# A two-layer encoder trunk: the order of the opening, four float32 products, and one more seven-product chunk

## The chip, the cores and the metric

The kernel runs on one core of one Trainium2 chip. The metric is device microseconds of one execution, lower is better; the time of a kernel is the median of its runs. The engines are TensorE (PE: products; PEld: its weight loads), VectorE (DVE), ScalarE (ACT), GpSimd (POOL) and SyncE (SP), whose queue issues nearly all the transfers.

## The reference, cut to what matters

```python
SEQ, D_MODEL, D_FF, DEPTH = 256, 1024, 2816, 2
def swiglu(h, w_gate, w_up, w_down):
    return (jax.nn.silu(h @ w_gate) * (h @ w_up)) @ w_down

for i in range(DEPTH):
    h = rmsnorm(x, ffn1_norm[i])
    x = x + 0.5 * swiglu(h, ffn1_w_gate[i], ffn1_w_up[i], ffn1_w_down[i])
    h = rmsnorm(x, mix_norm[i])
    proj = h @ w_in[i]                    # q, k, v of self attention, q of memory attention
    ...                                   # self attention (another kind in each layer), memory attention
    x = x + jnp.concatenate([o_s, o_m], axis=-1) @ w_out[i]
    h = rmsnorm(x, ffn2_norm[i])
    x = x + 0.5 * swiglu(h, ffn2_w_gate[i], ffn2_w_up[i], ffn2_w_down[i])
```

All data are float32. The four feed-forward blocks hold most of the work: 256 rows of x by three matrices of 1024 x 2816 each.

## The kernel before, in words

**Three passes for one product.** TensorE multiplies in the type fp32r. A matrix is split into `hi`, its cast to fp32r (ScalarE), and `lo`, the rest (VectorE: raw minus `hi`), and a product is the sum of three passes, hi by hi, lo by hi and hi by lo, each 128 x 128 by 128 x 512 (`dense`, L511, L514, L517). The weights come in chunks of 1 MB into one of three `raw` buffers and are split there in four units (`split_hi`, L338, and `split_lo`, L356), into one of four pairs of buffers (`hl_left`); x is transposed on TensorE (`prep_half`: four transposes L525 into `xtp`, scaled to `y` on VectorE at L557, split into `xh`, at L560, and `xl`, at L562), for each half `tb` of the 256 rows and each half `hf` of the 1024 columns.

**A feed-forward block** (`ffn`) goes through 11 groups of 256 hidden columns, gate and up side by side in 512. K = 1024 is cut into two chunks `c` of four K tiles `k`, so a group is two weight chunks, each 4 tiles x 2 halves of rows x 3 passes = 24 products, which collect in the two banks `gu`. `evac` makes the hidden values and turns them round through DRAM (`hb`, `hd`, `hr`). Two neighbouring groups (`pair`) are done by a scheme of seven products of sums in place of eight; its sums of x (`pair_forms`) overwrite `y`. Then comes the down projection, 11 chunks of 24 products into four banks `acc`.

**Seven-product chunks.** Down chunks listed in `SEVEN` do with 7 x 3 products what otherwise takes 8 x 3: VectorE forms four sums of weights (`wsum`, L350), and seven units are split in place of four; of the hidden values it forms four sums (`sf`, L681) and seven split forms (`h`, L690 and L694) in place of one `ht` (L665, L667). The first such chunk of a block has two `hi` and two `lo` buffers; the later ones are guests (`guest`): their last three units go to `gxh` and `gxl`, the room of the transposed x, free in a down projection. There is one such room (`xt_room`), given back by the seventh product of a guest.

**The order.** The schedule is manual. A planner in Python (`Flow`) walks through the products in the order written in `ffn` and `mixer`, keeps a clock with guessed durations, and emits the other engines' instructions as its threads' conditions and times come due; each engine then runs its own list in that order and waits on semaphores for data and buffers. The loader's guess of arrivals is `dma_free` and `LAT`. At the start TensorE runs `warm` products of the identity, which are not used.

Of the kernel before, what the change touches and what calls it, by code (L numbers as in the profile page):

```python
# [20 lines left out]
P = 128  # L21
# [19 lines left out]
T_MM = 0.216  # L41
# [101 lines left out]
def kernel(  # L143
# [41 lines left out]
    def load_x(tb, hf, queue=None):  # L185
        (queue or nc.sync).dma_start(out=xs[tb][:, hf * 512:(hf + 1) * 512],
                                     in_=x[0, tb * P:(tb + 1) * P, hf * 512:(hf + 1) * 512])

    load_x(0, 0)
    load_x(1, 0, nc.scalar)  # L190
# [18 lines left out]
    def loaded():  # L209
        n = len(late_loads)  # L210
        yield lambda: late_done[0] >= n
        yield flow.now + 8.0
# [34 lines left out]
    class Item:  # L247
# [27 lines left out]
    dma_free = [2.5]  # L275
# [10 lines left out]
    def loader():  # L286
        for i, c in enumerate(chunks):
# [4 lines left out]
            n = len(c.parts)  # L292
            for j, (dst, src) in enumerate(c.parts):
                nc.sync.dma_start(out=dst(c.raw), in_=src)
                dma_free[0] += 2.9 / n
                if i < 2 and j % 2:
                    for q in range((j - 1) * 4 // n, (j + 1) * 4 // n):
                        c.block[q] = dma_free[0] + LAT
                if i == 1 and j == 1:
                    load_x(1, 1)  # L300
                    dma_free[0] += 0.7
            c.arrive = dma_free[0] + LAT
# [39 lines left out]
    def split_lo():  # L342
        for i, it in enumerate(items):
# [8 lines left out]
            for src, q, w, dep in it.units:  # L352
                yield lambda: it.hit[q] is not None
                yield it.hit[q]
                yield calm_v(i)
                nc.vector.tensor_sub(it.part(1, q, w), src(), it.part(0, q, w).bitcast(F32))  # L356
                t = flow.dve(512 * w)
                it.lot[q:q + w] = [t] * w
            raw_left[0] += it.frees
# [17 lines left out]
    SEVEN = {(0, 1): (), (0, 2): (1, 4, 7), (1, 1): (1, 4, 7), (1, 2): (1, 4, 7)}  # L377
# [64 lines left out]
    def plan_ffn(l, nm, wg, wu, wd):  # L442
# [8 lines left out]
        work = [(g, c) for g in range(NG) for c in range(2)]  # L451
        if pair is not None:
# [70 lines left out]

    def turn(dst, src, flipped=False):
        nc.tensor.transpose(out=dst, in_=src, identity=flip if flipped else ident)  # L525
        return flow.pe(T_TR)
# [9 lines left out]
    class Xt:  # L536
        def __init__(self, keep=False):
# [7 lines left out]
            self.keep, self.y, self.ft = keep, {}, [None] * 4  # L545

    def prep_half(xt, tb, hf, gc, wait=0.0):
# [11 lines left out]
        yield flow.dve(512)  # L559
# [3 lines left out]
        if xt.keep:  # L563
            xt.y[tb, hf] = y
        else:
            g2.give()
# [51 lines left out]
    def ffn(l, nm, xt, gc_next):  # L618
# [151 lines left out]
        def pair_forms():  # L770

            yield lambda: len(xt.y) == 4 and g4.left >= 4
# [76 lines left out]
        if (l, nm) != (0, 1):  # L849
            for tb in range(2):  # L850
                for c in range(2):
                    plain_chunk(0, c, (tb,))
        else:
# [775 lines left out]
    def start_gain():  # L1629
# [5 lines left out]
        flow.dve(16)  # L1635
        warm(2)
        yield 4.6
        warm(5)
# [12 lines left out]
    table_hint(AF.Silu)  # L1651
# [67 lines left out]
```

## Time and profile before

| | |
|---|---|
| runs before | 955.98 us median of 3 (955.21 to 956.04) |
| the profiled execution | 955.69 us; its span, first to last instruction, 953.9 us |
| TensorE | busy 945.6 us (99% of the span), 4475 records |
| VectorE, ScalarE, GpSimd | busy 820.0 (86%), 587.0 (62%), 109.1 us (11%) |
| transfers | 204.04 MB, mean 214 GB/s |

Times in the profile count from the first instruction. A row of the timeline has start, duration, engine, line of the kernel, operation, output<-inputs, shape and count; in brackets stand the idle time of the engine before it and what ended that. A float32 product that is no transpose shows as two records. A product's record lasts longer than its place in the row of products, since neighbours overlap: the cost of one is the spacing of the starts.

### The profile page before, as it was taken

To read this page: it belongs to the slowest core of one execution; us is meant where nothing else is said; L and a number is where in the kernel's file an instruction comes from. 1 tells how busy PE (TensorE), PEld (TensorE's weight loads), DVE (VectorE), ACT (ScalarE), POOL (GpSimd) and SP (SyncE) were. 2 spreads that over 40 slices of the span, in tenths; PEclk is the share of its full clock that TensorE was granted. 3 is DMA by queue.
4 is the path that set the end of the run, shared out by engine and by line. 5 is a ranking of instruction groups with operands and counts; after the bars stand their busy time and mean duration, and the time that the engine had idled before them with its cause. 6 is when DMAs were issued, how large, how long until landed. Compare 5 with 4: busy or idle time off the path is not lost.

```text
span 953.9 us, 13334 instructions
## 1 busy us (share of the span) xinstructions
PE 945.6 (99%) x4475; PEld 774.1 (81%) x4475; DVE 820.0 (86%) x1483; ACT 587.0 (62%) x1121; POOL 109.1 (11%) x160
## 2 busy tenths in 40 slices
PE   9999999999999999999999999999999999999998
PEld 7888888887777888888888888888787778888886
DVE  7898978888777899979889899796999888999884
ACT  6556566677676746647546656564676865665650
POOL 1000057621210100000000000000434200000000
PEclk9999999999999999999999999999999999999999
DMA  8987799486525387887746679775641367588751
GB/s 265 289 263 236 224 354 296 158 276 210 177 90 177 97 266 225 262 287 219 245 146 219 208 226 288 247 253 166 196 158 57 121 214 228 183 275 276 239 197 45
DMA packets 169887, 204.04 MB, mean 214 GB/s; under 512 B 10137, under 2 KB 145114, under 8 KB 169818
## 3 DMA queue, kind: packets, MB, share of 16 engines
q1 hardware_dynamic: 169498, 202.78, 66.0%
q8 instruction: 35, 0.57, 0.3%
q10 hardware_dynamic: 320, 0.40, 0.1%
q14 instruction: 34, 0.28, 0.1%
HBM read 188.99 MB, written 14.16 MB: 213 GB/s over the span
## 4 chain that ended last, share of the span: by engine, by line
PE 90%; DVE 6%; DMA 2%; ACT 1%; issue 1%; SPq 0%; ACTq 0%; DVEq 0%
PE gu L517 13%; PE gu L514 13%; PE gu L511 13%; PE acc L511 9%; PE acc L517 9%; PE acc L514 9%; PE pair_m L511 3%; PE pair_m L514 3%; PE pair_m L517 3%; PE pj L517 2%; PE pj L511 2%; PE pj L514 2%; DVE lo L356 2%; PE S L1360 1%; DMA x<-in_x_dram 1%; PE AV L1441 1%
## 5 line engine op out<-in xcount | busy, mean ns | idle before, releaser
L338 ACT CAST hi<-raw 128x512 fp32r<-128x512 f32 (+1 forms) x467 | 336.3, 770 | 172.6 <-DMA raw<-in_ffn_w_up_dram 45.6
L356 DVE TENSOR_TENSOR lo<-raw,hi 128x512 fp32r<-128x512 f32 (+1 forms) x467 | 391.9, 875 | 35.5 <-ACT hi L338 35.4
L514 PE MATMUL gu<-lo,xh 128*128 128x512 f32 x576 | 224.7, 390 | 0.5 <-DVE lo L356 0.5
L517 PE MATMUL gu<-hi,xl 128*128 128x512 f32 x576 | 224.5, 390 | 0.4 <-DVE xl L562 0.4
L511 PE MATMUL gu<-hi,xh 128*128 128x512 f32 x576 | 224.4, 390 | 0.0
L517 PEld LDWEIGHTS gu<-hi,xl 128*128 128x128 f32 x576 | 108.1, 188 | 23.9 <-DVE xl L562 1.7
L514 PEld LDWEIGHTS gu<-lo,xh 128*128 128x128 f32 x576 | 108.1, 188 | 23.5 <-DVE lo L356 1.4
L511 PEld LDWEIGHTS gu<-hi,xh 128*128 128x128 f32 x576 | 108.2, 188 | 22.3
L517 PE MATMUL acc<-hi,ht 128*128 128x512 f32 x280 | 109.5, 391 | 0.0
L511 PE MATMUL acc<-hi,ht 128*128 128x512 f32 x280 | 109.2, 390 | 0.0
L514 PE MATMUL acc<-lo,ht 128*128 128x512 f32 x280 | 109.1, 390 | 0.0
L338 ACT CAST hi<-wsum 128x512 fp32r<-128x512 f32 x82 | 47.7, 619 | 26.5 <-DVE wsum L350 26.5
L514 PE MATMUL pj<-lo,xh 128*128 128x512 f32 x160 | 64.0, 400 | 0.0
L517 PE MATMUL pj<-hi,xl 128*128 128x512 f32 x160 | 63.8, 399 | 0.0
L511 PE MATMUL pj<-hi,xh 128*128 128x512 f32 x160 | 63.8, 399 | 0.0
L514 PEld LDWEIGHTS acc<-lo,ht 128*128 128x128 f32 x280 | 52.6, 188 | 10.9
L517 PEld LDWEIGHTS acc<-hi,ht 128*128 128x128 f32 x280 | 52.6, 188 | 10.8
L511 PEld LDWEIGHTS acc<-hi,ht 128*128 128x128 f32 x280 | 52.6, 188 | 10.7
L532 POOL TENSOR_TENSOR xr<-v,nhalf 128x1 f32<-128x1 f32 x12 | 10.3, 861 | 435.1 <-DVE v L530 435.1
L356 DVE TENSOR_TENSOR lo<-wsum,hi 128x512 fp32r<-128x512 f32 x82 | 52.8, 680 | 0.0
L633 ACT ACTIVATE sil<-gu,xr 128x256 f32<-128x256 f32 x72 | 33.7, 468 | 29.8 <-PE gu L517 29.7
L532 POOL TENSOR_TENSOR hf<-v,nhalf 128x8 f32<-128x8 f32 (+1 forms) x20 | 31.4, 1570 | 87.3 <-DVE v L530 78.9
(232 smaller groups left out, 1429.5 us busy)
## 6 DMA issues: line engine op xcount, KB each, us to landing
raw<-in_ffn_w_down_dram SPq DMA_DIRECT2D x176, 256.0 KB, 4.5
raw<-in_ffn_w_gate_dram SPq DMA_DIRECT2D x82, 512.0 KB, 4.0
raw<-in_ffn_w_up_dram SPq DMA_DIRECT2D x82, 512.0 KB, 5.4
raw<-in_w_in_dram SPq DMA_DIRECT2D x32, 512.0 KB, 4.4
hd<-hb SPq DMA_DIRECT2D x44, 256.0 KB, 4.6
hr<-hd SPq DMA_DIRECT2D x44, 256.0 KB, 4.6
raw<-in_w_out_dram SPq DMA_DIRECT2D x8, 1024.0 KB, 5.1
raw<-in_w_mem_kv_dram SPq DMA_DIRECT2D x4, 1024.0 KB, 5.3
```

The lines of the kernel that those rows point to most:

```text
L338: nc.scalar.copy(out=it.part(0, q, w), in_=src())
L356: nc.vector.tensor_sub(it.part(1, q, w), src(), it.part(0, q, w).bitcast(F32))
L511: nc.tensor.matmul(out=ps, lhsT=xh, rhs=wh, start=start, stop=False)
L514: nc.tensor.matmul(out=ps, lhsT=xh, rhs=wl, start=False, stop=False)
L517: nc.tensor.matmul(out=ps, lhsT=xl, rhs=wh, start=False, stop=stop)
L532: nc.gpsimd.tensor_tensor(out=dst, in0=v[:, :n], in1=nhalf[:, :n], op=ALU.pow)
L633: nc.scalar.activation(sil, ps[tb][:, 0:256], AF.Silu, scale=xt.r[tb])
L1360: nc.tensor.matmul(out=ss[e][:, pr, :nk], lhsT=q[rows, pr, :], rhs=k[rows, pr, :], start=i == 0, stop=i == len(passes) - 1)
L1441: nc.tensor.matmul(out=av[64 * e:64 * e + 64, pr, :], lhsT=vsrc(kb, pr, e), rhs=pts[e][:, pr, kb, :], start=(kb == 0), stop=(kb == nb - 1))
```

## The change

1. In the first block, the first halves of K of groups 0 and 1 come first: chunks (0,0), (1,0), (0,1), (1,1). The second halves of x are loaded behind the second weight chunk, and their preparation is due later.
2. K tiles 0 and 1 of the very first weight chunk are multiplied in float32, from `raw` and `y`, without split (`whole`): four products in place of twelve passes. Only tiles 2 and 3 of that chunk are split. `pair_forms` of this block waits until the fifth item.
3. Five of the eleven warm products go; one half of the first weight block is issued on ScalarE's queue, where the first x half of the second rows was, and that x block goes to SP's queue. The planner's guesses of the opening are changed.
4. In the last block, the seven-product chunks are 1, 3, 5, 7 in place of 1, 4, 7.

```diff
-            self.units = [(self.own(q, w), q, w, None) for q in range(0, 4, w)]
+            whole = 0 if items else 2
+            self.units = [(self.own(q, w), q, w, None) for q in range(whole, 4, w)]
...
-                nc.sync.dma_start(out=dst(c.raw), in_=src)
-                dma_free[0] += 2.9 / n
+                (nc.scalar if i == 0 and j == 1 else nc.sync).dma_start(out=dst(c.raw), in_=src)
+                dma_free[0] += 3.0 / n
...
-                if i == 1 and j == 1:
-                    load_x(1, 1)
-                    dma_free[0] += 0.7
+                if i == 0 and j == 1:
+                    table_hint(AF.Silu)
+                    load_x(1, 0)
+                    dma_free[0] += 0.75
...
-            if i == 0:
-                load_x(0, 1)
-                dma_free[0] += 0.7
+            if i == 1:
+                for tb in range(2):
+                    load_x(tb, 1)
+                    dma_free[0] += 0.75
...
-    SEVEN = {(0, 1): (), (0, 2): (1, 4, 7), (1, 1): (1, 4, 7), (1, 2): (1, 4, 7)}
+    SEVEN = {(0, 1): (), (0, 2): (1, 4, 7), (1, 1): (1, 4, 7), (1, 2): (1, 3, 5, 7)}
...
+        if (l, nm) == (0, 1):
+            work[:4] = [(g, c) for c in range(2) for g in range(2)]
...
+    def whole(ps, xt, tb, c, k):
+
+        flow.until(lambda: tb in xt.first)
+        y, t = xt.first[tb]
+        flow.at(max(t, c.raws[0].block[k] + 0.2))
+        nc.tensor.matmul(out=ps, lhsT=y[:, k, :], rhs=c.own(k)(), start=k == 0, stop=False)
+        c.uses -= 1
...
-            yield lambda: len(xt.y) == 4 and g4.left >= 4
+            yield lambda: len(xt.y) == 4 and g4.left >= 4 and ((l, nm) != (0, 1) or at[0] >= 5)
...
-            for c in range(2):
-                for ks in ((0, 1), (2, 3)):
-                    plain_chunk(0, c, range(2), ks)
-        work = work[2:]
+            open_[0] = [bank(f"gu{tb}", (P, 512)) for tb in range(2)], [None, None]
+            flow.spawn(evac(0, *open_[0]))
+            for tb in range(2):
+                for k in range(2):
+                    whole(open_[0][0][tb], xt, tb, plan[l, nm, "gu"][0, 0], k)
+            plain_chunk(0, 0, range(2), (2, 3))
+            work = work[1:]
...
+        yield 4.0
         warm(2)
-        yield 4.6
-        warm(5)
+        yield 5.6
+        warm(0)
...
-            flow.spawn(start(tb, hf, (3.4, 8.8, 5.6, 10.8)[2 * tb + hf]))
+            flow.spawn(start(tb, hf, (3.4, 12.6, 5.3, 13.4)[2 * tb + hf]))
```

How instructions stand on three queues, before and now (line, operation, output<-inputs with buffer numbers, size of the output). First TensorE's opening; `x_85` and `x_86` are the first and second 128 rows of x, `gu_151`, `gu_152` (now `gu_144`, `gu_145`) the banks of group 0. Before, behind the gain transpose:

```order
L1646 MATMUL warm<-ident 128x128 x2
L525 MATMUL xtp<-ident,x_85 128x128 x4
L1646 MATMUL warm<-ident 128x128 x5
L525 MATMUL xtp<-ident,x_86 128x128 x4
L511 MATMUL gu_151<-hi_0_168,xh_130 128x512
L514 MATMUL gu_151<-lo_0_169,xh_130 128x512
L517 MATMUL gu_151<-hi_0_168,xl_132 128x512
```

Now, at the same place:

```order
L548 MATMUL xtp<-ident,x_85 128x128 x4
L1678 MATMUL warm<-ident 128x128 x2
L538 MATMUL gu_144<-raw_110,y 128x512
L548 MATMUL xtp<-ident,x_86 128x128 x4
L538 MATMUL gu_144<-raw_110,y 128x512
L538 MATMUL gu_145<-raw_110,y 128x512 x2
L518 MATMUL gu_144<-hi_0_163,xh_131 128x512
```

The transposes of the first x block stand ahead of the warm products, and four float32 products from `raw` and `y` ahead of the first split one.

Next SP's queue, behind the first weight chunk (`raw_111` before, `raw_110` now); `raw_121` is the second chunk in issue order, `raw_127` and `raw_128` the third. Before:

```order
L294 DMA raw_111<-in_ffn_w_up_dram 128x256
L186 DMA x_85<-in_x_dram 128x512
L294 DMA raw_121<-in_ffn_w_gate_dram 128x2x256
L294 DMA raw_121<-in_ffn_w_up_dram 128x2x256
L186 DMA x_86<-in_x_dram 128x512
```

Now:

```order
L295 DMA raw_121<-in_ffn_w_gate_dram 128x2x256
L295 DMA raw_121<-in_ffn_w_up_dram 128x2x256
L186 DMA x_85<-in_x_dram 128x512
L186 DMA x_86<-in_x_dram 128x512
L295 DMA raw_128<-in_ffn_w_gate_dram 128x4x256
```

The second halves of x went behind the whole second chunk, whose other two pieces stand ahead of these rows; that chunk is now of group 1, and was the second half of K of group 0.

Last VectorE in the last down projection, from the splits of the first guest chunk on: chunk 4 before (`lo_0_9029`, `gxl_9032`, `gxl_9033`), chunk 3 now (`lo_0_8966`, `gxl_8969`, `gxl_8970`). Before:

```order
L356 TENSOR_TENSOR lo_0_9029<-raw_8933,hi_0_9028 128x512 x3
L356 TENSOR_TENSOR lo_0_9029<-wsum,hi_0_9028 128x512
L356 TENSOR_TENSOR gxl_9032<-wsum,gxh_9030 128x512 x2
L356 TENSOR_TENSOR gxl_9033<-wsum,gxh_9031 128x512
L356 TENSOR_TENSOR lo_0_9062<-raw_8962,hi_0_9061 128x512 x4
L356 TENSOR_TENSOR lo_0_9087<-raw_9005,hi_0_9086 128x512
L667 TENSOR_TENSOR ht<-hr,ht 128x512
```

Now:

```order
L359 TENSOR_TENSOR lo_0_8966<-raw_8769,hi_0_8965 128x512 x3
L359 TENSOR_TENSOR lo_0_8966<-wsum,hi_0_8965 128x512
L359 TENSOR_TENSOR gxl_8969<-wsum,gxh_8967 128x512 x2
L359 TENSOR_TENSOR gxl_8970<-wsum,gxh_8968 128x512
L359 TENSOR_TENSOR lo_0_9013<-raw_8913,hi_0_9012 128x512 x4
L353 TENSOR_TENSOR wsum<-raw_8942 128x512
L353 TENSOR_TENSOR wsum<-raw_8942,wsum 128x512
L708 TENSOR_TENSOR sf<-hr 128x128
L708 TENSOR_TENSOR sf<-sf,hr 128x128
```

Before, the splits of two plain chunks, 5 (`lo_0_9062`) and 6 (`lo_0_9087`), stand behind a guest; now those of one, chunk 4 (`lo_0_9013`), and then the sums of the next guest, chunk 5 (`raw_8942`), and of its hidden values.

More of the change, by code (lines that the diff above doesn't have):

```diff
@@ L183, with load_x @@
     xs = [const.tile([P, D], F32, name=f"x{tb}") for tb in range(2)]
-    def load_x(tb, hf, queue=None):
-        (queue or nc.sync).dma_start(out=xs[tb][:, hf * 512:(hf + 1) * 512],
-                                     in_=x[0, tb * P:(tb + 1) * P, hf * 512:(hf + 1) * 512])
+    def load_x(tb, hf):
+        nc.sync.dma_start(out=xs[tb][:, hf * 512:(hf + 1) * 512],
+                          in_=x[0, tb * P:(tb + 1) * P, hf * 512:(hf + 1) * 512])
     load_x(0, 0)
-    load_x(1, 0, nc.scalar)
     ident = const.tile([P, P], F32, name="ident")
@@ L211, in loaded @@
         yield lambda: late_done[0] >= n
-        yield flow.now + 8.0
+        yield flow.now + 14.0
     late_done = [0]
@@ L274 @@
     xt_room = [False]
-    dma_free = [2.5]
+    dma_free = [3.25]
     LAT = 1.5
@@ L292, in loader @@
             n = len(c.parts)
+            lat = LAT if i > 1 else 0.6
             for j, (dst, src) in enumerate(c.parts):
-                nc.sync.dma_start(out=dst(c.raw), in_=src)
-                dma_free[0] += 2.9 / n
+                (nc.scalar if i == 0 and j == 1 else nc.sync).dma_start(out=dst(c.raw), in_=src)
+                dma_free[0] += 3.0 / n
                 if i < 2 and j % 2:
                     for q in range((j - 1) * 4 // n, (j + 1) * 4 // n):
-                        c.block[q] = dma_free[0] + LAT
-                if i == 1 and j == 1:
-                    load_x(1, 1)
-                    dma_free[0] += 0.7
-            c.arrive = dma_free[0] + LAT
+                        c.block[q] = dma_free[0] + lat
+                if i == 0 and j == 1:
+                    table_hint(AF.Silu)
+                    load_x(1, 0)
+                    dma_free[0] += 0.75
+            c.arrive = dma_free[0] + lat
             c.block = [t or c.arrive for t in c.block]
-            if i == 0:
-                load_x(0, 1)
-                dma_free[0] += 0.7
+            if i == 1:
+                for tb in range(2):
+                    load_x(tb, 1)
+                    dma_free[0] += 0.75
             if i > 4 and late_done[0] < len(late_loads):
@@ L358, in split_lo @@
                 it.lot[q:q + w] = [t] * w
+            if i == 0:
+                yield lambda: whole_left[0] == 0
             raw_left[0] += it.frees
@@ L522, in dense @@
         return flow.pe(T_MM)
+    whole_left = [4]
+    def whole(ps, xt, tb, c, k):
[4 more added lines that the diff above has]
+        c.uses -= 1
+        whole_left[0] -= 1
+        if k == 1 and not xt.keep:
+            g2.give()
+        for _ in range(4):
+            flow.pe(T_MM)
+            flow.step()
     def turn(dst, src, flipped=False):
@@ L544, in __init__ @@
             self.done = [0, 0]
-            self.keep, self.y, self.ft = keep, {}, [None] * 4
+            self.keep, self.y, self.ft, self.first = keep, {}, [None] * 4, {}
     def prep_half(xt, tb, hf, gc, wait=0.0):
@@ L558, in prep_half @@
         banks.give()
-        yield flow.dve(512)
+        t = flow.dve(512)
+        opening = gc == GC_FFN1 and hf == 0
+        if opening:
+            xt.first[tb] = y, t
+        yield t
         nc.scalar.copy(out=xt.h[tb][:, ks, :], in_=y)
@@ L564, in prep_half @@
             xt.y[tb, hf] = y
-        else:
+        elif not opening:
             g2.give()
@@ L852, in ffn @@
                     plain_chunk(0, c, (tb,))
+            work = work[2:]
         else:
-            for c in range(2):
-                for ks in ((0, 1), (2, 3)):
-                    plain_chunk(0, c, range(2), ks)
-        work = work[2:]
+            open_[0] = [bank(f"gu{tb}", (P, 512)) for tb in range(2)], [None, None]
[5 more added lines that the diff above has]
+            work = work[1:]
         for w in work:
@@ L1650 @@
     warm(4)
-    table_hint(AF.Silu)
     flow.now = 2.7
```

## The prediction

> **What bounds the kernel now.** I read the page's engine shares first, then the chain of work that ended last, then who TensorE waited for, and then the timeline of the only two places that the change touches on purpose: the first 22 us and the last 50.
>
> ```profile
> PE 945.6 (99%) x4475; PEld 774.1 (81%) x4475; DVE 820.0 (86%) x1483; ACT 587.0 (62%) x1121; POOL 109.1 (11%) x160
> PE 90%; DVE 6%; DMA 2%; ACT 1%; issue 1%; SPq 0%; ACTq 0%; DVEq 0%
> PE warm L1646 <- POOL ident masks.py:199: 1.4, 1, 1.4
> ...
> PE gu L514 <- DVE lo L356: 0.5, 1, 0.5
> ...
> PE gu L517 <- DVE xl L562: 0.4, 1, 0.4
> PE xtp L525 <- DMA x<-in_x_dram: 0.3, 1, 0.3
> ```
>
> TensorE is the bound: busy 99% of the span and 90% of the chain. The waits name almost nothing; those on `gu` and `xtp` above all lie in the opening. So a product taken away anywhere saves its full spacing, and the opening is the one place with much idle time to fill. (Busy there overstates the work: overlapping records hide gaps, so I count products, not busy time.) The opening, as the timeline has it (start, duration, engine, line, operation, idle before and who ended it):
>
> ```profile
> 1.35 2.08 PE L1646 MATMUL warm<-ident 128*128 128x128 f32 x8 [1.35 <-POOL ident masks.py:199]
> ...
> 4.59 1.06 PE L525 MATMUL xtp<-ident,x 128*128 128x128 f32 x4
> ...
> 5.44 1.49 PE L1646 MATMUL warm<-ident 128*128 128x128 f32 x10
> ...
> 5.51 0.62 ACT L338 CAST hi<-raw 128x512 fp32r<-128x512 f32 x1 [2.36 <-DMA raw<-in_ffn_w_up_dram]
> 5.69 0.69 DVE L557 TENSOR_TENSOR y<-xtp,gcol 128x512 f32<-128x512 f32 x1 [1.83 <-PE xtp L525]
> ...
> 7.13 0.48 PE L511 MATMUL gu<-hi,xh 128*128 128x512 f32 x1
> ...
> 9.01 0.50 PE L514 MATMUL gu<-lo,xh 128*128 128x512 f32 x1 [0.48 <-DVE lo L356]
> ...
> 9.38 0.62 ACT L338 CAST hi<-raw 128x512 fp32r<-128x512 f32 x1 [1.30 <-DMA raw<-in_ffn_w_up_dram]
> ...
> 10.03 0.69 DVE L356 TENSOR_TENSOR lo<-raw,hi 128x512 fp32r<-128x512 f32 x1 [0.47 <-ACT hi L338]
> ...
> 10.06 0.66 PE L525 MATMUL xtp<-ident,x 128*128 128x128 f32 x4 [0.31 <-DMA x<-in_x_dram]
> ...
> 11.52 1.14 ACT L338 CAST hi<-raw 128x512 fp32r<-128x512 f32 x2 [0.37 <-DMA raw<-in_ffn_w_up_dram]
> ...
> 12.20 0.66 PE L525 MATMUL xtp<-ident,x 128*128 128x128 f32 x4
> ...
> 12.61 0.48 PE L514 MATMUL gu<-lo,xh 128*128 128x512 f32 x1
> ...
> 13.64 0.63 ACT L338 CAST hi<-raw 128x512 fp32r<-128x512 f32 x1 [0.46 <-DMA raw<-in_ffn_w_up_dram]
> ...
> 16.72 1.05 ACT L338 CAST hi<-raw 128x1024 fp32r<-128x1024 f32 x1 [0.80 <-DMA raw<-in_ffn_w_up_dram]
> ...
> 19.68 1.22 DVE L356 TENSOR_TENSOR lo<-raw,hi 128x1024 fp32r<-128x1024 f32 x1
> ...
> 21.13 0.39 PE L517 MATMUL gu<-hi,xl 128*128 128x512 f32 x1
> 21.36 0.39 PE L511 MATMUL gu<-hi,xh 128*128 128x512 f32 x1
> ```
>
> Two neighbouring products start 0.23 us apart (21.13 to 21.36; the page's 25 us slices hold 110 of them, so 0.227). The row at 21.36 is the first product of the third weight chunk. By then two chunks are done, 48 products of three passes, 2 x 24 x 0.227 = 10.9 us of work, and they began at 7.13: 14.2 us for 10.9, because the weights' K tile 3 (cast at 9.38) and the second halves of x (transposes at 10.06 and 12.20) came late. Those are the losses that the change goes for.
>
> **The change, part by part.**
>
> *Float32 products: the price of one.* The trace has no 128x512 float32 product. The nearest is the 128x128 one in the second mixer:
>
> ```profile
> 698.32 0.61 PE L1498 MATMUL AV<-V,PT 128*128 128x128 f32 x4
> 698.68 0.48 PE L517 MATMUL pj<-hi,xl 128*128 128x512 f32 x1
> 699.00 0.40 PE L511 MATMUL pj<-hi,xh 128*128 128x512 f32 x1
> ```
>
> From 698.32 to 699.00 lie four records, which are two float32 products, and one ordinary one: (0.68 - 0.227) / 4 = 0.113 per record, 0.227 per product of 128 columns, so 0.91 for 512 columns. Below, 0.68 (if it cost no more than the three passes it replaces); above, 1.04 (if each record of four times the length took the 0.13 of the spacing at 5.44, where the clock was still rising). I take 0.91: the AV row is the same operation at full rate. Four of them, 3.6 us, replace 12 passes, 2.7 us: 0.9 us more work. In return nothing has to be split before it: no cast at 5.51 and no `lo`, only y and the weights themselves.
>
> *The opening, step by step.* The transposes of the first x block now stand directly behind the small gain transpose, with the two warm products behind them: they start between 3.7 and the old 4.59, I take 3.8. Four take about 0.9 at the early rate; y follows (0.69), so y is ready near 5.6 (old: 6.38). The first weight block landed by 5.51 before; one half of it now goes out on ScalarE's queue in the place of an x block, at the same issue position, so it costs ScalarE nothing and lands no later. First float32 product at 5.7 (bounds 5.5 and 6.4). Then the second block's four transposes (0.4), and three more: 5.7 + 4 x 0.91 + 0.4 = 9.7; the early rate and the handover to y of the second block add some 0.3, so 10.0. K tile 2 is split by then. K tile 3 lands where it did, since the bytes ahead of it are the same (x block, x block, tiles 0 to 2): its `lo` is ready at 10.03 + 0.69 = 10.7, and TensorE wants it at 10.0 + 3 x 0.227 + 0.227 = 10.9. So 12 products follow nearly without a gap, to 12.9. The first half of K of group 1 moves ahead of the x halves on SP's queue: its tiles 0 and 1 lose one x block ahead of them, tiles 2 and 3 two. An x block cost 0.7 us there (13.64 - 11.52 = 2.1 for two weight pieces and an x), so casts near 10.8 and 12.2, `lo` near 12.1 and 13.5: in time for 12.9 and 14.3. The x halves now come behind, near 13 and 13.7, and their transposes stand inside group 1's first products; the 24 products take 5.45 and two groups of transposes 0.5 each (10.06 to the next product at 10.57 in the old order): 12.9 + 5.45 + 1.0 = 19.35 at the first product of the third chunk. Its bytes are the same as before, so cast at 16.7, `lo` (1.22 behind 1.05) at 19.0: just in time. Old 21.36, new 19.35: **-2.0 us**. Everything else that is moved here (the `pair` forms on VectorE wait until the fifth chunk, the gain columns come 6 us later on the planner's clock) lies under the products; VectorE, rid of two splits and, between 16 and 24 us, of the four y operations, has the easier time of it.
>
> *The last down projection.* Chunks 3 and 5 become seven-product ones in place of chunk 4: 21 passes instead of 24, once more: 3 x 0.227 = **-0.7 us** on TensorE. The price is paid on VectorE, between 877 and 933 us:
>
> ```profile
> L350 DVE TENSOR_TENSOR wsum<-raw,wsum 128x512 f32<-128x512 f32 x6 | 4.1, 686 | 0.1
> ...
> L356 DVE TENSOR_TENSOR gxl<-wsum,gxh 128x512 fp32r<-128x512 f32 x6 | 3.8, 684 | 0.0
> L667 DVE TENSOR_TENSOR ht<-hr,ht 128x512 fp32r<-128x512 f32 x4 | 2.7, 686 | 3.7 <-ACT ht L665 3.7
> ...
> L694 DVE TENSOR_TENSOR h<-sf,h 128x512 fp32r<-128x512 f32 x1 | 0.7, 684 | 0.0
> ...
> L681 DVE TENSOR_TENSOR sf<-hr 128x128 f32<-128x128 f32 x2 | 0.6, 283 | 0.0
> L694 DVE TENSOR_TENSOR h<-hr,h 128x256 fp32r<-128x256 f32 x1 | 0.4, 419 | 0.0
> ...
> 907.00:917.00 10.00, 10.00 (x46) 8.29 (x45) 9.93 (x21) 6.00 (x12) 0.00 (x0) 1.00 0.85 274
> 917.00:927.00 10.00, 10.00 (x46) 8.29 (x45) 9.94 (x17) 5.93 (x11) 0.00 (x0) 1.00 0.50 169
> ...
> 929.22 2.18 ACT L338 CAST hi<-raw 128x512 fp32r<-128x512 f32 x4 [3.25 <-PE acc L517]
> 929.88 2.50 DVE L356 TENSOR_TENSOR lo<-raw,hi 128x512 fp32r<-128x512 f32 x4 [2.94 <-ACT hi L338]
> 936.69 0.39 PE L514 MATMUL acc<-lo,ht 128*128 128x512 f32 x1
> ```
>
> One more such chunk is four `wsum` (4 x 0.686), three more `lo` (3 x 0.684), four `sf` (4 x 0.283) and three `h` in place of one `ht` (0.684 + 0.419 + 0.283 - 0.686): 2.74 + 2.05 + 1.13 + 0.70 = 6.6 us, and VectorE is full: 9.93 and 9.94 of 10 us in its column of the two rows of windows (us, then the busy time of TensorE, its loads, VectorE, ScalarE). What covers it is its lead. The tightest is the last chunk: its first `lo` ends near 930.6 and is used at 936.69, a lead of 6.1 us; ahead of it VectorE idled 2.94 us, because ScalarE waited for a buffer that chunk 6's products free. So 6.1 + 2.9 - 6.6 - 0.7 (TensorE is earlier) = 1.7 us stay. The chunks 3, 5 and 7 also share one room (the tiles of the transposed x), so chunk 5 is split only when chunk 3's products are through: between lie chunk 4's 24 passes, 5.45 us, against one cast (0.62) and one `lo` (0.68), and later ones come each 0.62 us for 0.68 of products. No wait is added to the path, I hold.
>
> *The rest.* No other product is added or removed. The planner's order shifts a little in the first mixer, with two more places where small products stand between long ones; one such change cost 0.09 (698.68 to 699.00 is 0.32, not 0.227): +0.1 to +0.2.
>
> Sum against the profiled execution, 955.69 us: -2.0 - 0.7 + 0.15 = -2.55, 953.1. The runs' median, 955.98, is 0.3 above that execution; I say **953.2**.
>
> **Rivals.** *TensorE stays at its slow rate.* The rows at 1.35 and 5.44 show the rate rise: eight warm records in 2.08 us, then ten in 1.49. Five warm products go, and the float32 ones start 1.5 us earlier than useful work did. If the first two ran at half rate, they would cost 1.8 more (955.0); all four 3.6 (956.8). Against it: TensorE is as busy from 1.35 to 5.7 as it was. The Trainium skill ("TensorE: Matmul & The Clock Gate", Part 1, and Part 4 on PE-mode transpose) says that the array runs at half its clock until some 3.4 us of sustained work are over, and that transposes do not count as such work; by that rule the exchange of warm products for transposes could delay the rise by a window, and the trace, where both kinds stand ahead of it, doesn't decide.
>
> *The opening stays bound by arrival*: the weights of group 1 come no earlier than before (casts at 11.52 and 13.64). Then `lo` of its tile 2 ends near 15.0 where I want it at 14.3, tile 0 near 12.9, and with the x halves later still about 1.1 of the 2.0 us goes: 954.3. For it: the DMA waits in brackets at 9.38, 11.52, 13.64 and 16.72.
>
> *VectorE becomes the bound of the last projection.* If the shared room stops the splits of chunks 5 and 7 until VectorE's queue is full, its 6.6 us land on the path: 953.2 + 6.6 = 959.8, slower. It decides from the point where the leads fall under about 2 us, which is what I have left at the last chunk. Against it: two earlier down projections use the same room for chunks 4 and 7, and no wait on it stands among TensorE's.
>
> **Numbers.** 0.2% of 955.98 is 1.9 us, about what a measurement can tell from no change. My forecast, 952.0 to 954.0: 0.72. Arrival: 0.13, mostly within 0.2%. Clock: 0.10, within 0.2%, or just above before. VectorE: 0.05, slower. Faster 0.74, same 0.20, slower 0.06. The range, 952.0 to 955.0, takes in the arrival case and half of the clock's; below, float32 products as cheap as three passes (-0.9).
>
> **What would show it.** Right: the float32 products (their line, `gu<-raw,y`) start near 5.7 and about 0.9 us apart; first product of the third chunk near 19.3; no wait of TensorE on `lo` or `gxl` behind 880; three products fewer there. Wrong: float32 records of 0.9 us each at the start (clock), TensorE idle on a DMA at 10 to 15 us (arrival), TensorE waiting for VectorE behind 900.

## The result, and the profile after

| | before | after |
|---|---|---|
| median of the runs | 955.72 us of 6 (955.21 to 956.04) | 961.11 us of 6 (958.77 to 963.28) |
| the profiled execution, and its span | 955.69, 953.9 us | 959.35, 957.6 us |

The changed kernel is slower: ratio 1.0054, 95% interval [1.0042, 1.0066]. Predicted were 953.2 us and a gain. The runs also scatter by 4.5 us, where the six of before keep within 0.9 (its longer series beside the experiments below spread over 3 to 5 us). One execution of run 13 below, the one that was profiled, took 1924.42 us, twice the others, and is left out there. (Line numbers of after: `hi` L341, `lo` L359, three passes L518, L521, L524, transposes L548, the float32 products L538.)

Engine shares, the chain by engine, and three of TensorE's waits, of after:

```profile
PE 945.6 (99%) x4458; PEld 772.3 (81%) x4458; DVE 825.0 (86%) x1494; ACT 589.9 (62%) x1124; POOL 114.2 (12%) x160
PE 75%; DVE 10%; DMA 8%; ACT 3%; SPq 2%; issue 2%; DVEq 0%; ACTq 0%
PE xtp L548 <- DVE x L633: 2.5, 1, 2.5
PE ptp L548 <- DVE pe L1453: 1.4, 1, 1.4
PE gu L521 <- DVE lo L359: 0.7, 2, 0.4
```

TensorE is as busy as before, 99%, yet only 75% of the chain is its own, where it was 90%: VectorE, transfers, ScalarE and SyncE's queue now carry a quarter. And the waits name VectorE three times, none of them in the opening. The opening of after:

```profile
3.94 1.11 PE L548 MATMUL xtp<-ident,x 128*128 128x128 f32 x4
4.84 1.06 PE L1678 MATMUL warm<-ident 128*128 128x128 f32 x4
5.83 1.93 PE L538 MATMUL gu<-raw,y 128*128 128x512 f32 x2
7.60 0.60 PE L548 MATMUL xtp<-ident,x 128*128 128x128 f32 x4
...
10.41 0.80 PE L518 MATMUL gu<-hi,xh 128*128 128x512 f32 x1
...
18.33 2.36 DVE L359 TENSOR_TENSOR lo<-raw,hi 128x1024 fp32r<-128x1024 f32 x2 [0.26 <-ACT hi L341]
...
19.91 0.39 PE L518 MATMUL gu<-hi,xh 128*128 128x512 f32 x1
```

The last row is the first product of the third chunk: 19.91, before 21.36. The opening does gain, 1.45 us. To see where it goes, I matched the same instructions of both kernels in program order and took the difference of their starts (after minus before): -1.5 at 22 us, -1.7 at 70 and at 100, -0.5 at 113, **+2.4 at 178**, and +4.9 from 300 to 600, behind the first mixer. From there on nothing is lost: the second mixer gives 1.0 back and the last down projection 0.7; the profiled spans differ by 3.7. So the loss lies between 100 and 300 us, in the rest of the first feed-forward block and the first mixer, where the change edits one condition (of `pair_forms`) and one wait of the planner (8.0 to 14.0 behind the late small loads).

Near 111, a split and the product that needs it (the same gate-up chunk, between two products of the pair), first of before, then of after, with a second wait 2 us on:

```profile
104.51 1.22 DVE L356 TENSOR_TENSOR lo<-raw,hi 128x1024 fp32r<-128x1024 f32 x1
...
111.99 0.39 PE L514 MATMUL gu<-lo,xh 128*128 128x512 f32 x1
```
```profile
109.49 1.22 DVE L359 TENSOR_TENSOR lo<-raw,hi 128x1024 fp32r<-128x1024 f32 x1
...
110.76 0.50 PE L521 MATMUL gu<-lo,xh 128*128 128x512 f32 x1 [0.28 <-DVE lo L359]
...
112.83 0.50 PE L521 MATMUL gu<-lo,xh 128*128 128x512 f32 x1 [0.41 <-DVE lo L359]
```

VectorE's **lead**, from the end of the first `lo` of a chunk to its use, was 111.99 - 105.73 = 6.3 us, the lowest of before from 35 us to 150. Now it is 0.05. TensorE came 1.2 us earlier, but VectorE came 5.0 later. At the end of the block, before and then after (TensorE's transposes of the new x wait for `x<-acc` on VectorE):

```profile
172.67 2.70 DVE L356 TENSOR_TENSOR lo<-raw,hi 128x512 fp32r<-128x512 f32 x4
175.89 0.69 DVE L606 SCALAR_TENSOR_TENSOR x<-acc,x 128x512 f32<-128x512 f32 x1 [0.52 <-PE acc L517]
...
177.73 0.60 PE L525 MATMUL xtp<-ident,x 128*128 128x128 f32 x4
```
```profile
176.72 2.69 DVE L359 TENSOR_TENSOR lo<-raw,hi 128x512 fp32r<-128x512 f32 x4
...
177.19 0.39 PE L524 MATMUL acc<-hi,ht 128*128 128x512 f32 x1
179.34 0.68 DVE L633 SCALAR_TENSOR_TENSOR x<-acc,x 128x512 f32<-128x512 f32 x1
180.07 0.66 PE L548 MATMUL xtp<-ident,x 128*128 128x128 f32 x4 [2.49 <-DVE x L633]
```

Before, VectorE had 0.52 us to spare ahead of `x`; now `x` stands behind a weight split that ends 4 us later, and TensorE starts nothing for 2.88 us. VectorE isn't short of time: between 90 and 140 us it idles more than before. It is late, and it waits for what ScalarE and the loads give it. SyncE's queue, of before and of after, shows where:

```profile
98.81 0.38 SPq L294 DMA_DIRECT2D raw<-in_ffn_w_gate_dram  x1
...
101.89 0.38 SPq L294 DMA_DIRECT2D raw<-in_ffn_w_gate_dram  x1
...
107.19 0.37 SPq L656 DMA_DIRECT2D hr<-hd  x1
```
```profile
102.40 0.38 SPq L295 DMA_DIRECT2D raw<-in_ffn_w_gate_dram  x1
...
103.98 0.38 SPq L683 DMA_DIRECT2D hr<-hd  x1
104.40 0.50 SPq L677 DMA_DIRECT2D hd<-hb  x1
110.04 0.36 SPq L683 DMA_DIRECT2D hr<-hd  x1
110.50 0.79 SPq L677 DMA_DIRECT2D hd<-hb  x1
111.33 1.10 SPq L295 DMA_DIRECT2D raw<-in_ffn_w_gate_dram  x1
```

The first load in each is that of the chunk for which TensorE waits: 3.6 us later, since its buffer comes free later. The second is the last gate-up chunk. Before, it was issued ahead of `hr<-hd`, the second half of a round trip of h through DRAM. Now two of these and two first halves stand ahead of it, and the second `hr<-hd` holds the queue for 5.1 us until its write has landed: 111.33 in place of 101.89. The lead of that chunk falls from 9.0 to 1.4 us, and what follows on VectorE up to `x` is later too.

### The profile page after: what moved, and what is told of

It is laid out like the page before. It is cut to its first block, busy times and chain, and to the rows that moved or that the text cites. A ratio compares the mean times of both kernels' runs of the same rounds, so it can differ in the third digit from the quotient of the medians.

```text
span 957.6 us, 13301 instructions
## 1 busy us (share of the span) xinstructions
PE 945.6 (99%) x4458; PEld 772.3 (81%) x4458; DVE 825.0 (86%) x1494; ACT 589.9 (62%) x1124; POOL 114.2 (12%) x160
## 4 chain that ended last, share of the span: by engine, by line
PE 75%; DVE 10%; DMA 8%; ACT 3%; SPq 2%; issue 2%; DVEq 0%; ACTq 0%
PE gu L524 10%; PE gu L521 10%; PE gu L518 10%; PE acc L518 7%; PE acc L524 7%; PE acc L521 7%; DVE lo L359 5%; DMA raw<-in_ffn_w_up_dram 3%; PE pj L524 3%; PE pj L518 3%; PE pj L521 3%; DMA raw<-in_ffn_w_down_dram 2%; PE pair_m L521 2%; PE pair_m L524 2%; PE pair_m L518 2%; SPq L295 2%
## 5 line engine op out<-in xcount | busy, mean ns | idle before, releaser
L341 ACT CAST hi<-raw 128x512 fp32r<-128x512 f32 (+1 forms) x464 | 334.5, 770 | 169.5 <-DMA raw<-in_ffn_w_up_dram 50.7
L359 DVE TENSOR_TENSOR lo<-raw,hi 128x512 fp32r<-128x512 f32 (+1 forms) x464 | 389.9, 878 | 30.5 <-ACT hi L341 30.2
L521 PE MATMUL gu<-lo,xh 128*128 128x512 f32 x572 | 223.2, 390 | 0.7 <-DVE lo L359 0.7
L518 PE MATMUL gu<-hi,xh 128*128 128x512 f32 x572 | 223.5, 391 | 0.0
L524 PE MATMUL gu<-hi,xl 128*128 128x512 f32 x572 | 223.0, 390 | 0.4 <-DVE xl L589 0.4
L521 PEld LDWEIGHTS gu<-lo,xh 128*128 128x128 f32 x572 | 107.4, 188 | 23.7 <-DVE lo L359 1.5
L524 PEld LDWEIGHTS gu<-hi,xl 128*128 128x128 f32 x572 | 107.4, 188 | 22.9 <-DVE xl L589 0.8
L518 PEld LDWEIGHTS gu<-hi,xh 128*128 128x128 f32 x572 | 107.4, 188 | 22.5 <-ACT hi L341 0.2
L524 PE MATMUL acc<-hi,ht 128*128 128x512 f32 x272 | 106.5, 392 | 0.0
L518 PE MATMUL acc<-hi,ht 128*128 128x512 f32 x272 | 106.2, 391 | 0.0
L521 PE MATMUL acc<-lo,ht 128*128 128x512 f32 x272 | 106.2, 390 | 0.0
L341 ACT CAST hi<-wsum 128x512 fp32r<-128x512 f32 x83 | 49.0, 619 | 38.9 <-DVE wsum L353 38.9
L518 PE MATMUL pj<-hi,xh 128*128 128x512 f32 x160 | 64.0, 400 | 0.0
L521 PE MATMUL pj<-lo,xh 128*128 128x512 f32 x160 | 64.0, 400 | 0.0
L524 PE MATMUL pj<-hi,xl 128*128 128x512 f32 x160 | 63.9, 399 | 0.0
L555 POOL TENSOR_TENSOR xr<-v,nhalf 128x1 f32<-128x1 f32 x12 | 11.2, 939 | 423.4 <-DVE v L553 423.4
L521 PEld LDWEIGHTS acc<-lo,ht 128*128 128x128 f32 x272 | 51.1, 188 | 10.7 <-DVE lo L359 0.2
L518 PEld LDWEIGHTS acc<-hi,ht 128*128 128x128 f32 x272 | 51.1, 188 | 10.4
L524 PEld LDWEIGHTS acc<-hi,ht 128*128 128x128 f32 x272 | 51.1, 188 | 10.4
L359 DVE TENSOR_TENSOR lo<-wsum,hi 128x512 fp32r<-128x512 f32 x83 | 53.5, 681 | 0.0
L663 DVE SCALAR_TENSOR_TENSOR h<-gu,xr,sil 128x256 f32<-128x256 f32 x72 | 34.4, 478 | 11.6 <-ACT sil L660 11.6
```

Source lines behind the costliest of these rows:

```text
L341: nc.scalar.copy(out=it.part(0, q, w), in_=src())
L518: nc.tensor.matmul(out=ps, lhsT=xh, rhs=wh, start=start, stop=False)
L521: nc.tensor.matmul(out=ps, lhsT=xh, rhs=wl, start=False, stop=False)
L524: nc.tensor.matmul(out=ps, lhsT=xl, rhs=wh, start=False, stop=stop)
L555: nc.gpsimd.tensor_tensor(out=dst, in0=v[:, :n], in1=nhalf[:, :n], op=ALU.pow)
L663: nc.vector.scalar_tensor_tensor(out=h, in0=ps[tb][:, 256:512], scalar=xt.r[tb], in1=sil, op0=ALU.mult, op1=ALU.mult)
```

## The experiments

Each ran in five rounds beside the kernel before on the same chip; ratios are to that kernel, with 95% intervals. The first four share a kernel before of 956.00 us.

**1. The opening alone**: the changed kernel with

```diff
-(1, 2): (1, 3, 5, 7)}
+(1, 2): (1, 4, 7)}
```

> The changed kernel with three seven-product chunks in the last down projection, as before: the opening alone. If the loss lies in the first block, whatever its cause, it stays, and the 0.7 us that the aligned traces show at the end go: about 961.8 (959.5 to 964, since the changed kernel's own runs lie from 958.8 to 963.3). If the seven-product chunks were the loss, it falls to about 954.

963.05 us, 1.0072 [1.0055, 1.0090]. The loss is the opening's.

**2. The seven-product chunks alone**: the kernel before with the reverse edit.

> The kernel before with chunks 1, 3, 5 and 7 as seven-product ones in the last down projection, and nothing else. Three passes of 0.227 us fewer: 955.0 against 955.7. If VectorE became the bound there (my rival): up to 6.6 more, 959 to 962.

955.20 us, 0.9990 [0.9982, 0.9999]: 0.8 us gained where 0.7 was predicted (the matched starts give 0.7 in that projection), and TensorE waits for nothing there, so VectorE covers it.

**3. Without the delay of the pair forms**

```diff
-yield lambda: len(xt.y) == 4 and g4.left >= 4 and ((l, nm) != (0, 1) or at[0] >= 5)
+yield lambda: len(xt.y) == 4 and g4.left >= 4
```

> The changed kernel without the condition that the pair forms wait for the fifth chunk (at[0] >= 5): VectorE makes them as soon as y is there, as before. Theory A, that this delay shifted VectorE's, SyncE's and ScalarE's order behind 36 us and ate VectorE's lead: the stalls at 110, 112 and 177 us go, the opening's 2.0 and the end's 0.7 stay: 953.0 (952.5 to 954). Theory B, that any shift of the opening upsets the order that is written out behind it: no better than 958 to 963. Theory C, the gain columns and rope tables coming 6 us later on the planner's clock: the same 958 to 963.

961.67 us, 1.0056 [1.0044, 1.0068]: theory A, as it stood, falls. The time is lost elsewhere now, in the opening (VectorE, TensorE, and a row of windows with TensorE's granted clock behind the four busy times and GpSimd's):

```profile
19.09 2.87 DVE L807 TENSOR_TENSOR y<-y 128x512 f32<-128x512 f32 x4
21.88 1.22 DVE L359 TENSOR_TENSOR lo<-raw,hi 128x1024 fp32r<-128x1024 f32 x1
```
```profile
20.89 0.39 PE L518 MATMUL gu<-hi,xh 128*128 128x512 f32 x1
23.15 0.50 PE L521 MATMUL gu<-lo,xh 128*128 128x512 f32 x1 [1.87 <-DVE lo L359]
```
```profile
24.00:28.00 4.00, 4.00 (x13) 2.94 (x12) 3.97 (x7) 2.71 (x5) 1.76 (x2) 0.62 0.30 73
```

The forms stand ahead of the third chunk's split, which TensorE now wants at once. It idles 1.87 us, and then gets half rate: granted clock 0.62 over 24 to 28 us. So the condition protects the opening. Behind it theory A has a part of its due: there is no wait for `x` at 177 us any more (matched starts +5.0 from 130 us to 200). And the condition isn't free, as the next run shows.

**4. The delay of the pair forms alone**: the kernel before with that condition added.

> The kernel before with that condition alone added, nothing else of the opening changed. Theory A: the same stalls without the gain of the opening, 958 to 963, slower than 955.7. Theory B or C: 955.7 within 0.5, since the opening, its transfers and the gain columns are as before.

956.16 us, 0.9998 [0.9990, 1.0007]: no loss. But look at the same split and product as above:

```profile
108.84 1.22 DVE L356 TENSOR_TENSOR lo<-raw,hi 128x1024 fp32r<-128x1024 f32 x1
...
111.98 0.39 PE L514 MATMUL gu<-lo,xh 128*128 128x512 f32 x1
```

The lead is 111.98 - 110.06 = 1.9 us. The condition alone takes 4.3 of the 6.3 us of lead and costs nothing. Of the 1.9 us that are left, a TensorE that comes 1.2 us earlier takes most.

The next four share a kernel before of 955.49 us.

**5. The planner's wait behind the small loads back**

```diff
-        yield flow.now + 14.0
+        yield flow.now + 8.0
```

> The changed kernel with the planner's wait after the late small loads (gains, positions, lambda) put back from 14.0 to 8.0. Theory C, that the 6 us later gain columns and rope tables fill VectorE and GpSimd at the end of the first block and in the mixer: the wait of 2.9 us at 177 and the 1.8 us lost between 178 and 246 go, the 1.2 us at 110 and 112 stay: about 957 (956 to 958.5). Theory D, that VectorE's and SyncE's order is upset as a whole by the opening, with no single term: 960 to 963 as without it.

961.54 us, 1.0059 [1.0043, 1.0074]. Theory C doesn't explain the loss. In its profile the first mixer costs only 0.6 us in place of 2.5 (matched starts +4.4 at 200 us, +4.9 at 300). But TensorE waits 2.7 us for `lo` in the first block, where it waited 0.7, so the total stays.

**6. That wait alone**, 8.0 to 14.0 in the kernel before.

> The kernel before with that wait raised from 8.0 to 14.0 and nothing else. Theory C: a wait at the end of the first block and some in the mixer, 957.5 to 960, slower than 956.0. Theory D: 956.0 within 0.5.

957.68 us, 1.0020 [1.0010, 1.0030]: it costs 2.2 us where nothing else is wrong, and the matched starts put it in the mixer (+0.2 at 200 us, +2.1 at 300). I had costed it at nothing.

**7. Both in the kernel before.**

> The kernel before with both: the pair forms after the fifth chunk and the wait of 14.0; the opening as before. If these two terms together, without the float32 products, make the loss: 958 to 961. If the loss needs TensorE's earlier start, which takes the last 2 us of VectorE's lead: 956 to 957, and VectorE's lowest lead between 100 and 130 us stays 1 to 3 us.

957.24 us, 1.0015 [1.0006, 1.0024]. Condition and wait together give a third of the loss, no more than the wait alone gave in run 6, and the lowest lead is 1.9 us, as expected; the rest needs the new opening.

**8. The round trip of h on another queue**

```diff
-            nc.sync.dma_start(out=hd.rearrange(...
+            nc.gpsimd.dma_start(out=hd.rearrange(...
-            nc.sync.dma_start(out=hr, ...
+            nc.gpsimd.dma_start(out=hr, ...
```

> The changed kernel with the round trip of h through DRAM (hd<-hb and hr<-hd, L677 and L683) issued from GpSimd's queue in place of SyncE's, so that no weight load stands behind a round trip that isn't there yet. Theory E, that this order on SyncE's queue (the load at 111.33 stands behind hr<-hd, which waits 5.1 us for the write) makes the loads late and eats VectorE's lead: no wait on lo between 90 and 130, the wait at 177 smaller, 955 to 958. Otherwise: 960 to 964, or more if GpSimd's own work delays the round trip.

956.74 us, 1.0010 [0.9997, 1.0023]: 4.4 us of the loss are gone, with the order on VectorE, ScalarE and TensorE unchanged. The profiled execution took 953.48 us, the fastest of the twelve, and no wait on `lo`, `x` or `pe` is left in it. SyncE's queue:

```profile
98.90 0.37 SPq L295 DMA_DIRECT2D raw<-in_ffn_w_gate_dram  x1
...
101.99 0.37 SPq L295 DMA_DIRECT2D raw<-in_ffn_w_gate_dram  x1
```

The load that came at 111.33 comes at 101.99, the lowest lead from 35 to 150 us is 3.05, and the matched starts keep -1.7 at 100 us and -2.5 at the end. That is the predicted time, from nearly the predicted terms: 1.7 us in the opening and 0.7 in the last projection. That the two mixers cancel in between (1.0 us lost, 1.1 gained) is luck. And the runs go from 953.5 (mean granted clock 1.000) to 960.1 (0.996), so something else differs from run to run.

The next four share a kernel before of 956.04 us.

**9. The control: that queue in the kernel before.**

> The kernel before with the round trip of h (hd<-hb, hr<-hd) issued from GpSimd's queue, nothing else: the control. Theory E, that the order on SyncE's queue costs only where VectorE's lead has been used up: nothing to gain, 955.5 within 0.5. If the other queue is simply better everywhere (the later blocks too): 954.5 or less, and then the gain of 4.4 us that the changed kernel had from it says nothing of the change.

956.56 us, 1.0007 [0.9996, 1.0019]: no gain, and above the range expected. But the control isn't a clean one, since its profile has a wait of TensorE that before's has not:

```profile
85.27 0.24 PE L231 MATMUL gps<-ident,grow 55*128 55x55 f32 x1 [1.57 <-DMA raw<-in_ffn_w_up_dram]
```

This product transposes the gain rows (`grow`). In before the load of the last of these was issued at 78.29 us and had landed when the product's turn came, near 83.8. With the round trip on the other queue the load was issued at 80.93 and landed at 84.92, and TensorE stood for 1.57 us. So the queue may give the kernel before something that this wait takes away again; that the change is worth nothing there by itself is not shown.

**10. Queue and wait** (8 with 5).

> The changed kernel with the round trip of h on GpSimd's queue and the wait of 14.0 back at 8.0. The 14.0 alone cost the kernel before 2.2 us, in the mixer: if that is a term of its own, 954.5 (953.5 to 955.5). If it only upset that kernel's order: 956.7 as without.

955.26 us, 0.9991 [0.9983, 1.0000]: in the range expected, 1.5 us better than run 8. The profile is of its slowest execution (956.43 us), and with the queue moved it still has two of the old waits:

```profile
PE xtp L548 <- DVE x L633: 1.5, 1, 1.5
PE gu L521 <- DVE lo L359: 0.8, 1, 0.8
```

In this execution TensorE got its full rate at 9.6 us, in run 8's at 7.4. So the other queue alone doesn't keep the waits away.

**11. Queue and an earlier start of TensorE**

```diff
+    wz = junk.bitcast(F32)[:, :P]
+    nc.vector.memset(wz, 1.0)
...
-    warm(4)
+    warm(6, wz)
```

> The changed kernel with the round trip of h on GpSimd's queue, and six warm products in place of the first four, on a tile that VectorE fills, so that TensorE starts some 0.5 us earlier (0.85 in place of 1.35). Theory F, that what is left of the loss (runs from 953.5 at a mean granted clock of 1.000 to 960.1 at 0.996) is TensorE at half rate in the opening, until a time that differs from run to run by some 2.5 us: about 0.5 lower, 956.2, and fewer runs over 959. Otherwise 956.7 with the same scatter.

953.84 us, 0.9980 [0.9969, 0.9990]: 2.9 us better than with the queue alone, where 0.5 was expected, and faster than before. No run is over 957. The opening of this run, and of run 5 (where nothing of the opening was edited):

```profile
1.05 2.93 PE L1681 MATMUL warm<-junk 128*128 128x128 f32 x12 [1.05 <-DVE junk L193]
...
4.72 0.61 PE L1681 MATMUL warm<-ident 128*128 128x128 f32 x4
5.67 1.12 PE L540 MATMUL gu<-raw,y 128*128 128x512 f32 x2 [0.34 <-DVE y L582]
6.63 0.60 PE L550 MATMUL xtp<-ident,x 128*128 128x128 f32 x4
```
```profile
4.83 1.06 PE L1678 MATMUL warm<-ident 128*128 128x128 f32 x4
5.82 2.08 PE L538 MATMUL gu<-raw,y 128*128 128x512 f32 x2
7.68 1.06 PE L548 MATMUL xtp<-ident,x 128*128 128x128 f32 x4
```

Four warm records take 0.61 us in the one and 1.06 in the other: full and half rate. With the early start every float32 product runs at full rate. In run 5 even the transposes at 7.68 take 1.06, and by the trace's record of the granted clock full rate came at 9.87 us. In the seven profiles with the changed opening (after, runs 1, 3, 5, 8, 10, 18) it came at 7.4, 7.5, 9.4, 9.6, 9.8, 9.9 and 10.0 us; in six of before's opening at 5.4 to 7.6, ahead of its first products or close behind.

The opening alone doesn't explain all 2.9 us. Ahead of the first full rate the record reads 1.00 (run 5's windows from 5 to 9 us do, in which the rows show half rate), so a mean granted clock says nothing of the opening: 0.996 stands for some 7 to 8 us at half rate later on (0.004 x 958 / 0.5). Run 8 has three executions with 0.998 or less, run 11 has none under 0.999. So with the early start TensorE also stays at full rate behind the opening; what keeps it there was not traced. And the two profiled executions take 953.75 us with full rate at 4.4 and 953.48 (run 8) with 7.4.

**12. All three.**

> All three: the round trip on GpSimd's queue, the wait of 8.0, the six early warm products. With the opening's gain, the tables' 2.2 us and part of the clock: 954.0 (953 to 955), 1.5 us under the kernel before. If the terms don't add up: 956 to 957.

953.72 us, 0.9981 [0.9966, 0.9997]: level with run 11, so the 1.5 us of run 10 and the 2.9 of run 11 don't add. Its profile shows one reason: with the wait of 8.0 the product of the gain rows stands at 85 us and waits 1.0 us for its load, as in run 9; with 14.0 (run 8) it stands at 91 us.

The next four share a kernel before of 955.96 us.

**13. The earlier start alone**, without the queue.

> The changed kernel with only the six early warm products (no change of queue). With the round trip on GpSimd's queue they were worth 2.9 us. Clock and queue as separate terms: 958.2 (957.5 to 959.5). If TensorE's earlier start is eaten by the stalls behind it, because VectorE's lead is already gone: 960 to 961.5, little better than the changed kernel's 961.1.

960.91 us (median of six), 1.0047 [1.0031, 1.0063]: worth nothing by itself. That TensorE waits out behind the opening what it gains there fits, but is not shown: none of these six was profiled.

**14. Its control in the kernel before.**

> The kernel before with the six early warm products, the control of the clock term. Its products start at 7.13 us, when its TensorE had full rate in most profiles (5.4 to 7.6): 955.8 (955.3 to 956.2), nothing to gain. If early warm products help any kernel by 2.9 us: 953.

957.03 us, 1.0007 [0.9995, 1.0018]: nothing to gain, though 0.8 us above the range expected.

**15. The two warm products ahead of the first transposes again**

```diff
-        yield 4.0
         warm(2)
```

> The changed kernel with its two warm products put back ahead of the first transposes of x, where the kernel before has them, and nothing else. If what delays the full rate is that the transposes stand ahead of warm products, the full rate comes between 5.4 and 7.6 again in place of 7.4 to 10, while y and the first float32 product come some 0.7 us later: 960 (959.5 to 960.5). If the order doesn't matter to the clock: 961.8, since only the delay is left.

963.74 us, 1.0071 [1.0049, 1.0094]. Both numbers expected are missed, and the trace of its slowest execution (967.83 us) says why. Its opening was the best of the unrepaired ones: full rate at 5.1 us, and 1.9 us ahead of before at 100 us, where after is 1.7 ahead. Then (timeline, and windows as above):

```profile
184.15 1.12 PE L548 MATMUL xtp<-ident,x 128*128 128x128 f32 x4 [3.62 <-DVE x L633]
```
```profile
176.00:183.00 7.00, 4.53 (x20) 3.35 (x19) 7.00 (x16) 5.87 (x12) 6.09 (x12) 0.97 0.81 273
183.00:189.00 6.00, 4.85 (x14) 3.99 (x15) 4.73 (x12) 1.24 (x3) 4.94 (x13) 0.50 0.80 271
...
244.00:247.00 3.00, 3.00 (x10) 1.99 (x12) 2.44 (x7) 2.16 (x5) 0.00 (x0) 0.51 0.18 61
```

The wait at the end of the block grew to 3.6 us, and TensorE came out of it at half rate (0.50 from 183 to 189 us), and once more after a wait in the mixer. A half-rate stretch of 3.4 us costs a busy TensorE 1.7. Such stretches would make mean clock and time go together, and in the six runs of after they do, from 1.000 (span 957.0 us) to 0.996 (961.5); the one of them with a trace has no such stretch before its last two us, so for the others this is inferred. Nor is half rate all of run 15's loss: three of its six executions have a mean clock of 1.000 and take 960.4 to 964.4 us.

**16. What the new opening is worth**: the kernel before with the queue, the early start and the chunks 1, 3, 5, 7.

> The kernel before with everything that helped or was free of the new opening: round trip on GpSimd's queue, six early warm products, chunks 1, 3, 5 and 7 as seven-product ones. Against it the changed kernel with the same (953.7) shows what the new opening is worth by itself. If it is worth the 2.0 us that the trace shows: 955.3 (954.8 to 956). If nothing: 953.7.

956.76 us, 1.0007 [0.9996, 1.0018], slower than either case expected. Against 953.72 with the new opening that is 3.0 us by the medians and 2.5 by the ratios, on two chips. It overstates the opening: what was added here for the queue costs this kernel a wait of 1.3 us for the gain rows, as in run 9. Against run 2, the kernel before with the four seven-product chunks alone (955.20 us, 0.9990), run 12 is 1.5 us faster by the medians and 0.9 by the ratios, and their intervals overlap.

The last two ran beside a kernel before of 955.91 us.

**17. Run 15 with the queue.**

> The changed kernel with the two warm products back ahead of the first transposes (as in the run that took 963.7, where the opening was 3.1 us ahead of the kernel before and the wait at 177 us grew to 3.6 and was followed by TensorE at half rate) and the round trip of h on GpSimd's queue. If a better opening only makes the later wait longer, and that wait alone turns the gain into a loss: with the wait gone 953.5 to 954.5. If the order of warm products itself is bad: 958 or more.

958.03 us, 1.0024 [1.0014, 1.0034]: 5.7 us better than run 15, but not 953.5. In its profile the full rate came only at 10.8 us, the opening was level with before, TensorE waited on `lo` at 112 and 114 again, and at the block's end there was a gap of 1.2 us (matched starts +0.2 at 100 us, +2.8 at 178). With the two warm products ahead, TensorE idles 0.78 us for y; the order of the warm products is no repair. And with a late opening the waits are back even with the queue moved, as in run 10.

**18. The memory tokens' preparation later**

```diff
-            if (l, nm) == (0, 1) and c == 2:
+            if (l, nm) == (0, 1) and c == 5:
                 flow.spawn(memory_prep())
```

> The changed kernel with the preparation of the memory tokens (meml, L1043) started three chunks of the down projection later (c == 5 in place of 2): 6 of these operations in place of 24 stand on VectorE ahead of the first x<-acc. If VectorE is late there through its own work: 18 times 0.30 = 5.4 us less ahead of x, the wait of 2.9 us at 177 goes, 957 to 958.5 where the changed kernel has 961.1. If it is late because its loads are: the work that is taken away was waiting time, and the wait stays, 960 to 962.

965.14 us, 1.0096 [1.0074, 1.0118]. Its waits:

```profile
PE xtp L548 <- DVE x L633: 3.7, 1, 3.7
PE kv L524 <- DVE meml L1043: 3.6, 2, 2.1
```
```profile
171.38 2.79 DVE L359 TENSOR_TENSOR lo<-raw,hi 128x512 fp32r<-128x512 f32 x4 [3.31 <-ACT hi L341]
```

With 18 operations less ahead of it, `x` is no earlier: the wait is 3.7 us. VectorE stood idle for 3.31 us ahead of the splits of the second last chunk. It was late through what it waits for, not through its own work. The work moved away became a wait of its own, 3.6 us in the mixer.

## Why the prediction was wrong

*The step that failed* is the sentence "Everything else that is moved here ... lies under the products; VectorE ... has the easier time of it". It took busy time for slack. VectorE had less to do, but it was later: its lead, 6.3 us at the tightest, paid 4.3 us for the delayed pair forms (run 4) and 1.2 for the earlier TensorE, and the rest went in late loads. In after TensorE then waits for VectorE 0.7 us on `lo`, 2.5 on `x` and 1.4 on `pe`. I had worked out leads in the last projection, where VectorE is full, and not in the first block, where it idles. Shown is that SyncE's queue has a large part in it: with the round trip of h moved away and the order on VectorE, ScalarE and TensorE the same, the load is 9.3 us earlier, these waits go, and 4.4 us come back (run 8). That it is the whole cause is not shown: the waits return where the full rate comes late (runs 10 and 17), and the control (run 9) has a wait of its own.

*The opening* was right in its mechanism. The float32 products begin at 5.83 (predicted 5.7), the ordinary ones at 10.41 (10.0), the third chunk at 19.91 (19.35). At full rate the records of the float32 products start 0.43 us apart (after: 9.52, 9.95, 10.38), so a product of two records costs 0.86 us, near the 0.91 predicted. The gain was 1.45 us of 2.0 with full rate at 7.5, when the first of the four ran at half rate; it is 2.0 at the same place with full rate at 4.4 (run 11). (The sum should have ended at 953.4, 953.1 plus the 0.3 by which the median lies above the profiled execution, and not at 953.2.)

*The rival "TensorE stays at its slow rate"* had 0.10 and came true in part: in five of seven profiles the first two of the four float32 products ran at half rate, and the ordinary ones began at 11.2 to 11.4 us in place of 9.4 (run 11), about the 1.8 us that the prediction put on this case. By its sum that gives 955.0; it alone wouldn't have made the kernel slower. The Trainium skill ("TensorE: Matmul & The Clock Gate", Part 1) explains the steps: the rate is set by a free-running window of 3.41 us, so when it rises depends on where in the window the work begins. The trace agrees: the half-rate stretches of run 15 last 6.83 and 3.41 us.

Whether transposes count as work was left open, and the runs don't settle it. The Trainium skill ("TensorE: Matmul & The Clock Gate", Part 4 on PE-mode transpose) says that they don't count in the same way. Counted back from the five late rises (9.4 to 10.0), the window that failed began at 2.6 to 3.1 us and held the transposes of the gains and of x (3.5 to 4.9), while TensorE was busy for 3.1 to 3.3 of its 3.41 us, which fits. But in after the window from 178.16 to 181.57 us kept the full rate with 1.50 us of work, some of it transposes (180.07 to 180.48), and in run 3 one with 1.55 us and no transposes lost it. There the transposes seem to have counted. No run here changes them alone.

*The other rivals*: arrival (the third chunk is 0.56 us later than forecast) was small; VectorE as the bound of the last projection did not happen (run 2).

*The last projection* was right: 0.8 for 0.7 us (run 2).

*The gain columns and tables 6 us later* I costed at nothing under cover of the products. Alone they cost 2.2 us, in the mixer (run 6).

*What stays open*: whether the other queue helped by order alone or by its own path, since the two halves of the round trip took 3.8 and 4.6 us in the median there (run 8), 5.2 and 5.1 on SyncE's (after), which is 1.9 us of the 9.3 by which the load came earlier; what the queue gives the kernel before without the wait for the gain rows; and why a late opening (runs 10 and 17) shrinks VectorE's lead more than it delays TensorE.

## What to carry to other kernels

Where each engine runs a list that was ordered beforehand, read the lead of every supplier over its user, chunk by chunk, before you move the user earlier: a gain is only worth what the smallest lead behind it allows, and a change that takes lead costs nothing until another comes. Look for transfers that wait inside an in-order queue ahead of loads. Look at the profile of a control too, since it can have a wait of its own. And two repairs may each show nothing, or half, where both together give the gain: early warm products were worth 0 us with the queue blocked and 2.9 with it free.

## What the runs showed of the hardware

Short gaps can drop the rate: a gap of 2.26 us between two starts on TensorE (run 3, 20.89 to 23.15) was followed by 3.41 us at half rate, while one of 2.88 us (after, 177.19 to 180.07) was not. The place of the gap matters: counted in steps of 3.41 us from the first full rate, run 3's gap lies in one step, which leaves 1.55 us of work there, and after's reaches over an edge, which leaves 2.83 and 1.50. Why 1.55 lost the rate and 1.50 kept it stays open. The Trainium skill ("TensorE: Matmul & The Clock Gate", "Why this matters for your kernels") warns of gaps above some 3 us; here 2.3 were enough once.

Starting TensorE 0.3 us earlier (1.05 in place of 1.35, with 12 unbroken records) moved the full rate from between 7.4 and 10.0 us to 4.3 and 4.4 in the two profiles of the changed opening (runs 11 and 12): a whole window for a third of a microsecond. It is no guarantee: with before's opening it came at 4.1 in one profile (run 14) and at 7.1 in another (run 16).
